# Late eigenvalue powers four to seven on GpSimd in the half-block loop of an S5 layer

## The chip, the cores and the metric

The kernel runs on one core of a Trainium2 chip. The core has a TensorE (PE, with its weight loads shown as PEld), a VectorE (DVE), a ScalarE (ACT) and a GpSimd (POOL); transfers are issued from the queues of SyncE (SP), ACT and GpSimd. Each engine runs its own instructions in order, and the engines wait for one another by semaphores. The metric is the device time of one launch in microseconds; with several runs, the median counts.

## The reference

One layer over 1024 latent tokens and 256 context tokens with 1024 channels: an S5 mixer (64 groups of 16 channels, 64 complex states each, two directions, the latent scan starting from the context's final state), GELU and a gated linear unit, then a SwiGLU feed-forward, with RMS norms and modulation by a condition. Cut to what matters here:

```python
def s5_direction(u_ctx, u_lat, lam_re, lam_im, log_step, b_re, b_im, c_re, c_im):
    lam = lax.complex(lam_re, lam_im)
    lam_bar = jnp.exp(lam * jnp.exp(log_step)[:, None])
    b_bar = ((lam_bar - 1.0) / lam)[..., None] * lax.complex(b_re, b_im)
    c_mat = lax.complex(c_re, c_im)

    def run(u, h0):
        bu = jnp.einsum('lgh,gnh->lgn', u, b_bar)
        bu = bu.at[0].add(lam_bar * h0)
        a = jnp.broadcast_to(lam_bar, bu.shape)
        _, h = lax.associative_scan(_linear_combine, (a, bu), axis=0)
        return jnp.einsum('lgn,ghn->lgh', h, c_mat).real, h[-1]

    y_c, h_c = run(u_ctx, zeros)
    y_l, _ = run(u_lat, h_c)
    return y_c, y_l
```

## The kernel before

Time is cut into chunks of T = 8 tokens (32 context chunks, 128 latent ones). Inside a chunk everything is matrix products with powers of the eigenvalues, `lam_bar` to the 1st up to the 8th, kept in `PW` (eight complex rows of 64 groups on 128 partitions: both directions times 64 states). From chunk to chunk runs a scan over the chunk states.

**The half-block loop** (`for hb in range(16)`, from line 698) makes these chunk states. The 64 groups are eight blocks of eight; a half block is one block in one direction. For each half block there is

- `bl_make`: two products of the input matrix with the powers, two 128x1024 instructions, on GpSimd for the half blocks in `PMUL` (1, 3, 5, 6, 8, 10, 13) and on the VectorE for the others; made six half blocks ahead;
- `bl_sum` (L433): the two products added, by an accumulating DMA that GpSimd's queue issues; five half blocks ahead. Since the queue is in order, this issue waits there until both products exist;
- `bl_tr` (L443): eight transposes on PE, copied to SBUF by ACT (L446), with `bb_copy` (L451); two half blocks ahead;
- `sums` (L584): 32 products on PE, in two halves of 16, copied by ACT (L590, L592, L593) into the states `STQ`, four buffers of 20 KB per partition in the region `RA`;
- `pair`: the states combined two by two, in four 128x256 instructions, on GpSimd (temporaries `ptmp`, KB 2 and 3 of the region `RXc`) for the half blocks in `PPAIR`, else on the VectorE; one half block later;
- `u_ctx`, `rs_lat`, `u_act`: the input's norm and modulation, on GpSimd (the context of a block, two 128x256 instructions), VectorE and ACT. `UCTX` says in which half block which block's context comes; `sums(8)` is the first to use block 4;
- `ctx_tree` on the VectorE: the scan over the 32 context chunks.

`sums`, `bl_tr` and `pw_full` take their PSUM banks from one ring of two (`pv2`). The order of all this is written out by hand: the order of the source is the order in each engine's queue.

**The powers.** Before the loop the VectorE makes the rows 0, 1, 3 and 7 of `PW` (powers 1, 2, 4, 8). Row 2 (power 3) is `pw_mul(PW[:, 2:3], ...)` in half block 3, rows 4, 5 and 6 (powers 5, 6 and 7) come from two calls in half block 4. A call is four GpSimd instructions: two products into two temporaries, a subtraction and an addition. `pw_full(0)` and `pw_full(1)` turn rows 0 to 3 and 4 to 7 on PE (eight products, L386), and ACT copies the result to `PWF` (L388), which is first read by the output matrices `cl_ops` on GpSimd from half block 12 on. `PW` shares its place with the end of the last state buffer, which `sums(12)` is the first to write, and the temporaries of `pw_mul` lie in the third state buffer, which `sums(8)` is the first to write.

**Behind the loop** come the last `pair` on GpSimd, the rest of the output matrices, `ctx_last`, and the scan over the latent chunks (`scan`, on the VectorE, one step after another), beside which GpSimd and PE make output matrices and Toeplitz kernels (`k_mats`, turned by a DMA through DRAM into `KQ`). Then follow the mixer's output, the gated unit and the feed-forward.

Of the kernel before, what the change touches and what calls it, by code (L numbers as in the profile page):

```python
# [24 lines left out]
G = 64  # L25
# [17 lines left out]
def s5_ffn_kernel(tc, a, out):  # L43
# [3 lines left out]
    with ctx:  # L47
        ctx.enter_context(tc.manual_schedule())
        sb = ctx.enter_context(tc.tile_pool(name="sb", bufs=1))
        def region(tag, kb, dt=F32):  # L50
            return sb.tile([P, int(kb * 256)], dt, tag=tag, name=tag)

        def view(reg, kb, shape, parts=P):
            off = int(round(kb * 256))
            n = int(np.prod(shape))
            v = reg[:parts, off:off + n]
            if len(shape) > 1:
                names = "abcdef"[:len(shape)]
                v = v.rearrange(f"p ({' '.join(names)}) -> p {' '.join(names)}",
                                **{k: d for k, d in zip(names, shape)})  # L60
            return v
# [3 lines left out]
        RA = region("ra", 80.5)  # L65
        RU = region("ru", 40)
        RC = [region(f"c{i}", 16) for i in range(4)]
        RXa, RXc = region("rxa", 8), region("rxc", 8)
        RW = region("rw", 6)

        def bc(ap, axis, n):
            sh = list(ap.shape)
            sh.insert(axis, n)
            return ap.unsqueeze(axis).to_broadcast(sh)

        def tt(o, x, y, op, eng=V):
            eng.tensor_tensor(out=o, in0=x, in1=y, op=op)  # L77
# [69 lines left out]
        def pv2():  # L147
            return pW.tile([P, 2, 512], F32, tag="v", name="pv", bufs=2)
# [46 lines left out]
        def ada1(h, *ks):  # L195
            for k in ks:
                for b in range(2):
                    i = 2 * b + h
                    PE.matmul(prow[32 * i:32 * i + 2], scs[:, k], stage[h][k][:, b], start=k == 0, stop=k == 7, tile_position=(0, 32 * i))
# [141 lines left out]
        def pw_mul(o, x, y):  # L341

            m = x.shape[1]
            a_, b_ = (view(RA, kb, [m, 2, G]) for kb in (42, 43))
            yr, yi = (bc(bc(y[:, i], 1, 2), 1, m) for i in range(2))
            tt(a_, x, yr, MUL, E)
            tt(b_, x[:, :, ::-1], yi, MUL, E)
            tt(o[:, :, 0], a_[:, :, 0], b_[:, :, 0], SUB, E)
            tt(o[:, :, 1], a_[:, :, 1], b_[:, :, 1], ADD, E)
# [4 lines left out]
        def power8():  # L354

            pt = pv2()[:, 0, 0:128].rearrange("p (r q d e) -> p r q d e", r=2, q=8, d=2)
            for gp in range(2):
                for d in range(2):
                    sl = slice(64 * d, 64 * d + 64)
                    PE.matmul(pt[64 * gp:64 * gp + 64, :, :, d], ident[:, sl],  # L360
                              PW[:, 7].rearrange("p r (q e t) -> p r q e t", q=8, t=2)[:, :, :, :, gp], start=True, stop=True)
            pt = pt.rearrange("p r q d e -> p r (q d e)")
            S.copy(SQ[0][:, 0::2], pt)
            S.activation(SQ[0][:, 1], pt[:, 1], AF.Copy, scale=-1.0)
            S.copy(LQ[0], SQ[0])
# [16 lines left out]
        def pw_full(n):  # L382
            pt = pv2()[:, 0].rearrange("p (t i d a) -> p t i d a", t=4, i=2, d=2)
            for gp in range(2):
                for d in range(2):
                    PE.matmul(pt[64 * gp:64 * gp + 64, :, :, d], ident[:, 64 * d:64 * d + 64], PW[:, 4 * n:4 * n + 4, :, gp::2],  # L386
                              start=True, stop=True)
            S.copy(PWF[:, 4 * n:4 * n + 4], pt)  # L388
# [48 lines left out]
        def bl_tr(hb, copy=True):  # L437
            b, d = bd(hb)
            t1 = bls(hb)[0]
            pt, w_ = pv2(), Win[hb % 3]  # L440
            for j in range(2):
                for i in range(4):
                    PE.transpose(pt[:, j, P * i:P * i + P], t1[:, 4 * j + i].rearrange("p s h -> p (s h)"), ident)  # L443
            if not copy:
                return pt, w_
            S.copy(w_.rearrange("p j i n -> p (j i n)"), pt.rearrange("p j n -> p (j n)"))  # L446
            bb_copy(hb)
# [7 lines left out]
        def mix_rows():  # L455
            S.copy(r4, prow.rearrange("p (m n) -> p m n", m=4))

        def mix_turn():
            for m in range(4):
                PE.transpose(prow[:, P * m:P * m + P], r4[:, m], ident)  # L460

        def mix_scale(h):

            hs, pt = slice(4 * h, 4 * h + 4), prow.rearrange("p (m n) -> p m n", m=4)
            for r in range(2):
                tt(cb[:, r, :, hs], pt.rearrange("p m (b j q) -> p b j m q", b=2, j=2)[:, :, h, :, r], modb[:, 0:2, hs], ADD)
            stt(cb[:, :, 1, hs], cb[:, :, 1, hs], 1.0, bc(nrm[:, 0, hs], 1, 2), ADD, MUL)
            for r in range(2):
                tt(mx[:, r].rearrange("p b (j g) -> p b j g", g=T), bc(cb[:, r, :, hs], 3, T), bc(bc(msk, 1, 4), 1, 2), MUL)
# [107 lines left out]
        def sums(hb):  # L577
            b, d = bd(hb)
            for j in range(2):
                w, pv = Win[hb % 3][:, j], pv2()  # L580
                for ri in range(2):
                    for i in range(4):
                        c0 = 160 * (i // 2)
                        PE.matmul(pv[64 * (i % 2):64 * (i % 2) + 64, ri, c0:c0 + 160], w[:, i, 64 * ri:64 * ri + 64],  # L584
                                  U[:, 8 * b + 4 * j + i], start=True, stop=True)
                pv = pv[:, :, 0:320].rearrange("p r (e c) -> p c r e", e=2)
                e = 8 * (b % 2) + 4 * d + 2 * j
                st = STQ[b // 2][:, :, :, e:e + 2]
                if d == 0:
                    S.copy(st, pv)  # L590
                else:
                    S.copy(st[:, 159:31:-1], pv[:, 32:160])  # L592
                    S.copy(st[:, 31::-1], pv[:, 0:32])  # L593
# [88 lines left out]
        PPAIR = (3, 5, 7, 8, 9, 11, 12, 13, 15)  # L682
        UACT = {1: (2, 0, 4), 2: (2, 4, 8), 3: (3, 0, 4), 4: (3, 4, 8)}
        UACT.update({6 + i: (4 + i // 2, 4 * (i % 2), 4 * (i % 2) + 4) for i in range(8)})
        UCTX = {1: 2, 3: 3, 6: 4, 7: 5, 9: 6, 11: 7}
        RSL = {0: 2, 1: 3, 3: 4, 5: 5, 6: 6, 8: 7}
        ADA1 = {0: (0, 1), 1: (2, 3, 4), 2: (5, 6, 7)}
        ADA2 = {10: 12, 11: 14, 12: 16, 13: 18, 15: 22}
# [9 lines left out]
        for hb in range(16):  # L698
            sums(hb)
            ada1(1, *ADA1.get(hb, ()))  # L700
            if hb == 0:
                power8()
            if hb == 3:
                mix_rows()
            for n in BLTR.get(hb, (hb + 2,)):
                if n < 16:
                    bl_tr(n)
            if hb == 3:
                mix_turn()
            if hb == 4:  # L710
                mix_scale(1)
                mix_sel(1)
            if hb in RSL:
                rs_lat(RSL[hb])
            if hb == 4:
                mix_cols(1)
                tq = pA.tile([P, 512], F32, tag="r3", name="tq")
                LQ += [t[:, o_:o_ + 192].rearrange("p (r e) -> p r e", e=G) for t, o_ in ((tq, 0), (tq, 192), (LTb, 256))]
            if hb == 0:
                tt(Xc[:, 16:], ctxT[:, 16:], bc(rcp, 1, G - 16), MUL)  # L720
            if hb == 1:
                powers(0)
            if hb == 2:
                powers(1)
                SY.dma_start(BXY[:, 1], a["bxy"][:, 3])
            if hb in UACT:
                u_act(*UACT[hb])
            if hb in UCTX:
                u_ctx(UCTX[hb])
            if hb >= 1:  # L730
                pair(hb - 1, E if hb - 1 in PPAIR else V)
            if hb == 5:
                powers(2, 3)
            for a_ in CTREE.get(hb, ()):
                ctx_tree(*a_)
            if hb + 6 in (7, 9, 11, 12, 14, 15):
                lb_psum(hb + 6)
            bl_sum(hb + 5)
            bl_make(hb + 6)
            if hb == 3:  # L740
                pw_mul(PW[:, 2:3], PW[:, 0:1], PW[:, 1])
                tt(KD.rearrange("p q g h -> p (q g) h"), bc(pat, 1, 8), bc(dcol, 2, HC), MUL, E)
            if hb == 4:
                pw_mul(PW[:, 4:6], PW[:, 0:2], PW[:, 3])
                pw_mul(PW[:, 6:7], PW[:, 2:3], PW[:, 3])
            if hb in (6, 8):
                pw_full(hb // 2 - 3)
            if hb == 9:
                cs_load(0)
            if hb == 11:  # L750
                V.tensor_copy(LQ[4], SQ[4])
                cs_sign(0)
            for _ in range(CLAT.get(hb, 0)):
                CL0.pop(0)()
            ada_load(ADA2.get(hb, 0))
# [1004 lines left out]
```

## Time and profile before

| | us |
|---|---|
| median of 3 runs | 1024.42 (1023.78 to 1026.05) |
| the profiled execution | 1022.42 |
| its span, first to last instruction | 1020.6 |
| busy: PE, DVE, ACT, POOL | 961.9, 785.5, 436.5, 766.5 |
| loop, first sums to the last state copy | 40.0 to 122.4 |
| scan on the VectorE | 127.65 to 227.5 |

How to read it: a profile is one execution. A row of a timeline has the start, the duration, the engine, the line, the operation, the tile written and those read, the shape, the number of instructions merged into the row, and in brackets the idle time before it with what released it. Most helpers record their instructions at line 77 (`tt`), so the tiles tell them apart: `ru` is the input, `ra` holds states and powers, `rxc` the temporaries, `c` the four 16 KB regions, `pv` the PSUM ring. A row of waits has the waiting engine and line, what it waited for, the total, the number of times and the longest.

### The profile page before, as it was taken

The page shows a single profiled execution, that of the slowest core. Times are in us where ns is not written, and L with a number is a line of the kernel's source. Part 1 is how long each engine was busy: PE and PEld are TensorE (multiplying, and loading weights), DVE is VectorE, ACT ScalarE, POOL GpSimd, SP SyncE. Part 2 cuts the span into 40 slices and gives each one's busy share as a digit, 9 for nine tenths or more (in the row PEclk, how much of TensorE's full clock was granted, in tenths as well). Part 3 has the DMA queues.
Part 4 walks back from the last instruction along what each step waited for, and adds up shares of the span by engine and source line. Part 5 has one row for each costly group of instructions (what it writes and reads, how often), then busy time and mean ns, then how long its engine had stood idle before and what let it go on. Part 6 is the DMA issues. An engine that isn't in the chain of part 4 may idle for free. (4 is left out here: it accounts for less than half of the span.)

```text
span 1020.6 us, 18545 instructions
## 1 busy us (share of the span) xinstructions
PE 961.9 (94%) x6988; PEld 771.8 (76%) x6988; DVE 785.5 (77%) x1642; ACT 436.5 (43%) x854; POOL 766.5 (75%) x590
## 2 busy tenths in 40 slices
PE   5987798779999999999999999999999999999996
PEld 1466423668999987878888888888888888888885
DVE  7979799994365777997958768585958778686987
ACT  5477622234454663523334343424343343324337
POOL 5799899991682548979786877778686877777674
PEclk9999999989999999999999999999999999999999
DMA  9764997323612021011212112121212111121205
GB/s 335 276 139 91 298 341 231 91 74 89 227 61 83 2 104 62 22 42 42 83 41 74 39 45 62 42 73 52 73 42 82 39 40 58 42 73 52 73 22 165
DMA packets 48546, 98.95 MB, mean 97 GB/s; under 512 B 4285, under 2 KB 18877, under 8 KB 47177
## 3 DMA queue, kind: packets, MB, share of 16 engines
q1 hardware_dynamic: 43272, 86.64, 25.9%
q0 software_dynamic: 2016, 7.34, 3.8%
q10 hardware_dynamic: 3168, 3.79, 1.1%
q8 instruction: 55, 0.90, 0.4%
q14 instruction: 35, 0.28, 0.1%
HBM read 84.25 MB, written 6.17 MB: 89 GB/s over the span
## 5 line engine op out<-in xcount | busy, mean ns | idle before, releaser
L77 POOL TENSOR_TENSOR c<-rxc,c 128x512 fp32r<-128x512 f32 x128 | 170.0, 1342 | 55.6 <-ACT c L1227 53.7
L1286 PE MATMUL ut<-ra,c 128*128 128x512 f32 x400 | 155.8, 390 | 0.5 <-ACT ra L1227 0.3
L1287 PE MATMUL ut<-ra,c 128*128 128x512 f32 x400 | 155.7, 389 | 0.3 <-DVE ra L77 0.3
L1288 PE MATMUL ut<-ra,c 128*128 128x512 f32 x400 | 155.7, 389 | 0.0
L1227 ACT CAST c<-rxc 128x512 fp32r<-128x512 f32 x128 | 79.0, 622 | 146.4 <-PE xt L1568 51.8
L1568 PE MATMUL xt<-c,c 128*128 128x512 f32 x540 | 129.7, 389 | 0.0
L77 DVE TENSOR_TENSOR ru<-ru,xt 128x1024 f32<-128x1024 f32 x90 | 107.8, 1216 | 12.9 <-PE xt L1568 9.1
L1568 PEld LDWEIGHTS xt<-c,c 128*128 128x128 f32 x540 | 101.4, 188 | 21.0
L77 DVE TENSOR_TENSOR ru<-ut,ru 128x512 f32<-128x512 f32 x98 | 67.2, 686 | 42.4 <-PE ut L1288 36.9
L1286 PEld LDWEIGHTS ut<-ra,c 128*128 128x128 f32 x400 | 75.1, 188 | 16.7 <-ACT ra L1227 0.8
L1287 PEld LDWEIGHTS ut<-ra,c 128*128 128x128 f32 x400 | 75.1, 188 | 16.2 <-issue 0.6
L1288 PEld LDWEIGHTS ut<-ra,c 128*128 128x128 f32 x400 | 75.1, 188 | 15.9 <-POOL c L77 0.3
L77 POOL TENSOR_TENSOR c<-rw,c 128x512 fp32r<-128x512 f32 (+1 forms) x29 | 39.8, 1372 | 37.3 <-ACT c L1227 36.6
L77 POOL TENSOR_TENSOR c<-ru,c 128x512 fp32r<-128x512 f32 (+1 forms) x39 | 58.0, 1487 | 9.3 <-ACT c L1227 4.9
L1288 PE MATMUL ut<-c,c 128*128 128x512 f32 x160 | 62.4, 390 | 1.3 <-POOL c L77 1.3
L1287 PE MATMUL ut<-c,c 128*128 128x512 f32 x160 | 62.3, 389 | 0.0
L1286 PE MATMUL ut<-c,c 128*128 128x512 f32 x160 | 62.2, 389 | 0.0
L77 POOL TENSOR_TENSOR rxc<-rxc 128x512 f32<-128x512 f32 x40 | 60.9, 1523 | 1.6
L1568 PE MATMUL ut<-c,c 128*128 128x512 f32 x216 | 51.9, 389 | 0.0
L584 PE MATMUL pv<-ru,c 128*64 128x160 f32 x512 | 43.7, 312 | 7.3 <-POOL ru L77 2.6
L77 DVE TENSOR_TENSOR pe<-pe,ru 128x256 f32<-128x256 f32 x64 | 27.4, 429 | 29.5 <-ACT pe L1127 17.4
L77 DVE TENSOR_TENSOR ru<-ru,ut 128x512 f32<-128x512 f32 x76 | 47.3, 680 | 0.3
(427 smaller groups left out, 2568.2 us busy)
## 6 DMA issues: line engine op xcount, KB each, us to landing
c<-in_ada_w SPq DMA_DIRECT2D x46, 256.0 KB
rxc<-in_w SPq DMA_DIRECT2D x38, 256.0 KB
rxc<-in_w SPq DMA_DIRECT2D x19, 512.0 KB
ru<-in_w SPq DMA_DIRECT2D x11, 512.0 KB
rw<-in_w SPq DMA_DIRECT2D x11, 512.0 KB
ra<-in_ada_w SPq DMA_DIRECT2D x10, 512.0 KB
ra<-in_ada_w SPq DMA_DIRECT2D x18, 256.0 KB
ru<-in_xT SPq DMA_DIRECT2D x4, 1024.0 KB
```

Of the source, the lines that this page charges most:

```text
L77: eng.tensor_tensor(out=o, in0=x, in1=y, op=op)
L584: PE.matmul(pv[64 * (i % 2):64 * (i % 2) + 64, ri, c0:c0 + 160], w[:, i, 64 * ri:64 * ri + 64], U[:, 8 * b + 4 * j + i], start=True, stop= ...
L1227: S.copy(o[0], x)
L1286: PE.matmul(pu, wh, bh, start=start, stop=False)
L1287: PE.matmul(pu, wh, bl, start=False, stop=False)
L1288: PE.matmul(pu, wl, bh, start=False, stop=stop)
L1568: PE.matmul(pd, w[:, cs_], b, start=j in (1, 2, 4) and n == 0, stop=n == 2, skip_group_check=j not in (1, 2, 4))
```

## The change

`pw_mul` takes its temporaries from KB 2 and 3 of `RXc` instead of `RA`. Row 2 of the powers, and with it the instruction for the skip term `KD`, moves from half block 3 to 7; rows 4 to 6 move from 4 to 9; `pw_full(0)` and `pw_full(1)` move from the ends of half blocks 6 and 8 to those of 10 and 11. `u_ctx(4)` moves from half block 6 to 5. No instruction is added or taken away.

```diff
         def pw_mul(o, x, y):
 
             m = x.shape[1]
-            a_, b_ = (view(RA, kb, [m, 2, G]) for kb in (42, 43))
+            a_, b_ = (view(RXc, kb, [m, 2, G]) for kb in (2, 3))
...
-        UCTX = {1: 2, 3: 3, 6: 4, 7: 5, 9: 6, 11: 7}
+        UCTX = {1: 2, 3: 3, 5: 4, 7: 5, 9: 6, 11: 7}
...
             bl_sum(hb + 5)
             bl_make(hb + 6)
-            if hb == 3:
+            if hb == 7:
                 pw_mul(PW[:, 2:3], PW[:, 0:1], PW[:, 1])
                 tt(KD.rearrange("p q g h -> p (q g) h"), bc(pat, 1, 8), bc(dcol, 2, HC), MUL, E)
-            if hb == 4:
+            if hb == 9:
                 pw_mul(PW[:, 4:6], PW[:, 0:2], PW[:, 3])
                 pw_mul(PW[:, 6:7], PW[:, 2:3], PW[:, 3])
-            if hb in (6, 8):
-                pw_full(hb // 2 - 3)
+            if hb in (10, 11):
+                pw_full((10, 11).index(hb))
             if hb == 9:
                 cs_load(0)
```

## The prediction

> **What bounds the kernel now.** I began with the page, then the windows that follow the stages, then the waits of each engine in the half-block loop, and last the timeline of that loop engine by engine. The profiled execution took 1022.42 us, 1.8 us more than its span.
>
> ```profile
> span 1020.6 us, 18545 instructions
> ...
> 59.50:125.40 65.90, 51.63 (x529) 38.81 (x529) 52.44 (x145) 50.08 (x110) 64.41 (x82) 0.97 0.71 177
> 69.50:110.40 40.90, 33.00 (x334) 25.52 (x334) 38.90 (x101) 31.49 (x68) 39.80 (x56) 0.96 0.58 124
> 110.40:122.40 12.00, 9.62 (x109) 7.60 (x107) 5.28 (x20) 9.63 (x23) 11.84 (x14) 1.00 1.03 345
> 127.65:227.50 99.85, 83.63 (x1512) 48.12 (x1504) 97.75 (x508) 26.46 (x55) 96.80 (x66) 0.96 0.59 188
> 262.00:1020.60 758.60, 747.03 (x3736) 633.40 (x3730) 563.02 (x790) 314.74 (x617) 554.36 (x402) 1.00 0.19 61
> ```
>
> Columns after the length: busy PE, PEld, DVE, ACT, POOL, then granted clock, DMA share, GB/s. From 262 us the TensorE is full (747 of 759), so a delay at its start comes out at the end. From 127.65 to 227.5 the VectorE runs the serial scan without a pause, so a later start of the scan is a later end. The question is thus one number: how far does the start of the scan move? In the loop before it, GpSimd is full (64.4 of 65.9) and the VectorE nearly so until 110.4 (38.9 of 40.9); then the VectorE idles (5.3 of 12) and waits for states that PE and ACT make.
>
> ```profile
> DVE r L483 <- PE prow L476: 0.8, 1, 0.8
> ...
> PE pv L584 <- POOL ru L77: 2.6, 1, 2.6
> PE pv L584 <- ACT rxa L388: 1.8, 2, 0.9
> ...
> POOL rw L77 <- DMA c<-rw: 2.4, 1, 2.4
> ```
>
> The first row is the only wait of weight that the VectorE has between 69 and 111: nothing the change moves releases it. The second is PE waiting for the context of block 4 (two GpSimd instructions), the third PE waiting for the two copies of the eigenvalue powers. The last is GpSimd's only wait for anybody from 59 to 128, and it comes behind the loop.
>
> **GpSimd's queue, step by step.** Here are the rows of GpSimd that carry the change (start, duration):
>
> ```profile
> 68.61 1.84 POOL L77 TENSOR_TENSOR ra<-ra 128x128 f32<-128x128 f32 x4
> 70.41 0.40 POOL L77 TENSOR_TENSOR r<-r 128x128 f32<-128x128 f32 x1
> 70.77 1.29 POOL L77 TENSOR_TENSOR rxc<-ra,r 128x256 f32<-128x256 f32 x2
> ...
> 78.08 4.27 POOL L77 TENSOR_TENSOR ra<-ra 128x256 f32<-128x256 f32 x8
> 82.30 0.87 POOL L433 DMA_DIRECT2D c<-rxc  x1
> 82.91 1.60 POOL L77 TENSOR_TENSOR ru<-ru,r 128x256 f32<-128x256 f32 x2
> ...
> 89.37 0.88 POOL L433 DMA_DIRECT2D c<-c  x1
> ...
> 96.93 0.87 POOL L433 DMA_DIRECT2D c<-rxc  x1
> ...
> 101.84 0.88 POOL L433 DMA_DIRECT2D c<-c  x1
> 102.45 1.59 POOL L77 TENSOR_TENSOR rxc<-ra,r 128x256 f32<-128x256 f32 x2
> ...
> 105.46 0.88 POOL L433 DMA_DIRECT2D c<-c  x1
> ...
> 123.63 1.81 POOL L77 TENSOR_TENSOR ra<-ra,rxc 128x256 f32<-128x256 f32 x2
> ```
>
> From start to start, the four products of half block 3 take 1.80 us (68.61 to 70.41), the skip-term product behind them 0.36, the eight of half block 4 4.22 (78.08 to 82.30). All three, 6.38 us, leave their places. GpSimd would then reach the accumulating transfer of half block 12 (issued at 89.37) at 82.99; that block 4's context (82.91, 1.60) goes one half block ahead changes the order there, not this sum. But the transfer adds two operands that the VectorE makes:
>
> ```profile
> 85.23 2.35 DVE L77 TENSOR_TENSOR c<-c,tq 128x1024 f32<-128x1024 f32 x2 [0.19 <-issue]
> ```
>
> They are done at 85.23 + 2.35 = 87.58, and by the waits above nothing lets the VectorE be sooner. The issue sits in GpSimd's queue in order, so GpSimd now stands idle for some 4.6 us, until 87.6, and behind the waiting issue stand all its further products, pairs and transfers. Of 6.38 us taken out it keeps 1.77 as a lead. In half block 7 come back 1.80 + 0.36 (0.4 us late from there), in half block 9, behind the transfer of 14, the 4.22: from half block 10 on GpSimd is **4.6 us late**. It had no idle time left to make this good. Three things follow.
>
> First, the pairs. The last pair of the loop ended at 123.63 + 1.81 = 125.44; now 130.05. The scan's first addition reads what it wrote:
>
> ```profile
> 128.05 0.29 DVE L77 TENSOR_TENSOR ra<-ltb,ra 128x128 f32<-128x128 f32 x1
> ```
>
> So the scan starts at least 130.05 - 128.05 = 2.0 us later, whatever PE does.
>
> Second, the powers. Their second turn on PE with its copy moves from half block 8 to 11, between the transposes of 13 and the sums of 12, and it needs the eight products, which end where the pair of 102.45 begins: 102.45 + 4.6 = 107.05.
>
> ```profile
> 76.20 1.13 PE L386 MATMUL pv<-ra,r 128*64 128x256 f32 x8
> ...
> L388 ACT COPY rxa<-pv x2: 560/566/571, 79.0 to 92.1; 128x512 f32<-128x512 f32 x2
> ...
> 103.58 1.09 PE L443 MATMUL pv<-r,c 128*128 128x128 f32 x8 [1.07 <-ACT ra L593]
> 104.60 1.31 PE L584 MATMUL pv<-ru,c 128*64 128x160 f32 x16
> 109.81 1.06 PE L443 MATMUL pv<-r,c 128*128 128x128 f32 x8 [1.20 <-DMA c<-c]
> 114.40 1.09 PE L443 MATMUL pv<-r,c 128*128 128x128 f32 x8 [1.07 <-ACT ra L593]
> ...
> 108.16 1.27 ACT L590 COPY ra<-pv 128x640 f32<-128x640 f32 x2
> ```
>
> PE issues in order: with the transposes of 13 done near 103.7 it stands until 107.2, then 1.13 for the powers (108.3), then the sums of 12 in two halves of 1.31 (109.6 and 110.9; the second needs the bank that the copy of 0.57 frees, in time). The state copies of 12 end near 111.6 instead of 108.16 + 1.27 = 109.4, and the transposes of 14 start at 110.9 instead of 109.81: **+1.1** at full clock. From there PE and ACT hand each other two banks and the delay stays.
>
> But PE has stood still for 3.5 us. The one like gap in this loop (PE idle from 82 to 84) was followed by this:
>
> ```profile
> 82.00:84.00 2.00, 0.00 (x0) 0.00 (x0) 1.90 (x7) 1.94 (x5) 1.92 (x5) 1.00 0.17 33
> 84.00:86.00 2.00, 1.43 (x12) 1.28 (x14) 1.74 (x7) 0.82 (x3) 2.00 (x4) 0.52 1.03 197
> 86.00:88.00 2.00, 2.00 (x22) 1.85 (x20) 2.00 (x4) 0.72 (x1) 1.92 (x4) 0.63 0.22 41
> ...
> 84.57 3.80 PE L584 MATMUL pv<-ru,c 128*64 128x160 f32 x32 [2.60 <-POOL ru L77]
> ...
> 62.93 2.39 PE L584 MATMUL pv<-ru,c 128*64 128x160 f32 x32
> ```
>
> The granted clock fell to 0.52 and 0.63, and the same 32 products took 3.80 instead of 2.39: 1.4 us. With that the second path gives 1.1 + 1.4 = **+2.5**; I take it, since the new gap is longer than the one measured. The Trainium skill's page "TensorE: Matmul & The Clock Gate" (Part 1, the HAM clock gate) has the clock halved after about one free-running window of 3.4 us without work. By it a gap of 2.6 us need not have been enough, and the trace shows that it was. If by that rule the clock stays whole after the new gap, this path is +1.1, the pairs' +2.0 decides, and the time is 1026.4.
>
> Third, the accumulating transfers. That of 13 moves from 96.93 to 97.3, that of 15 from 105.46 to 110.05.
>
> ```profile
> DMA to landing us min/median/max: 4.5/5.3/8.8
> ...
> SPq L520 <- DMA c<-c: 4.5, 1, 4.5
> ```
>
> With the median of 5.3 the one of 15 lands at 115.4, before the transposes of 15 are due (114.40 + 1.1 to 2.5), so it costs nothing; with 8.8 it lands at 118.85, 4.45 after 114.40. The longest landings were under the modulation weights that SP loads from 102.6 on; but SP's queue then stands 4.5 us for this very landing, so a later transfer should find the DMA engines emptier, and I take the median. The Trainium skill's page "DMA: Bandwidth & Descriptors" (Anatomy of one DMA, SWDGE path) fits 2.0 us plus bytes over 436e3, an estimate of 3.2 us for these 512 KB. No landing here is under 4.5, so the measurement decides; by the page the larger rival below would vanish.
>
> **What I cost at nothing.** The context of block 4 now runs before PE needs it: this takes away the 2.6 us wait and 1.4 us of slow clock, and the powers' turns at 76 and 89 us free PE of 1.8 us of waits. PE runs ahead from half block 8, but the lead ends in half block 11, where the transposes of 13 need the transfer that lands at 97.3 + 5.3 = 102.6 (they began at 103.58), and then the powers; meanwhile the VectorE, full until 110.4, could not use it. The new temporaries are the two KB that GpSimd's own pairs use, in order on one engine: no wait. The same region is loaded again behind the loop by ACT's queue, which now waits for the last pair until 130.05; behind it on ACT stands a clearing copy that waited for the VectorE anyway. GpSimd's lateness also goes on into the output matrices; its wait of 2.4 for a transfer takes some of it.
>
> ```profile
> 214.39 3.92 PE L945 MATMUL pw<-ra,ru 128*128 128x128 f32 x16 [2.98 <-DMA ra<-kd]
> ...
> 227.66 0.49 PE L922 MATMUL pe<-c,ra 64*64 64x128 f32 x4 [1.55 <-DVE ra L77]
> ```
>
> There PE waits for kernels made from these matrices, and later 1.55 us for the scan: if all 4.6 us arrive, this path gives 4.6 - 1.55 = +3.05.
>
> **The sum.** Scan start +2.5 us, between +2.0 and +3.05: the profiled execution of the changed kernel 1022.42 + 2.5 = 1024.9. This profile lies 2.0 below the median of the runs, so the median goes from 1024.42 to **1026.9**, with 1026.4 to 1027.5 as this case's own range.
>
> **Rivals.**
> A larger loss: the transfer of 15 lands late (8.8 us), +4.45, and with a second slow clock of 1.4 after the wait +5.85: 1028.9 to 1030.3. For it: two loaded landings near 8 us. Against it: SP stands still then.
> No change: GpSimd's lag comes out smaller. The last pair may be 128.05 - 125.44 = 2.6 us late before the scan feels it; if the VectorE were done with its operands for half block 12 some 2 us sooner, or GpSimd's instructions ran quicker after its idle stretch, the time would be 1024.4. Against it: the VectorE has no wait there that could vanish.
> Faster: the early context is what decides. PE's 2.6 and 1.4 us at half block 8 are carried to the end of the loop: 1024.42 - 4.0 = 1020.4, or 1022.4 if half is. It decides if GpSimd issues the transfer of 15 before 105.46. For it: this is the longest wait of PE in the loop. Against it: GpSimd's queue, above, has 4.22 us of products ahead of that issue.
>
> **Numbers.** A difference under 0.2% (2.05 us) can't be told from none here. Forecast 0.60; its range lies at or above 1026.47, and I put 0.50 there and 0.10 below for the scatter of a median; larger loss 0.15; no change 0.12; faster 0.13. So slower 0.65, same 0.10 + 0.12 = 0.22, faster 0.13. The range runs from 1024.0 (no change) to 1030.0 (most of the larger loss) and leaves out the gain and a little of the loss.
>
> **What would show it.** In the changed profile: GpSimd idle for 4 to 5 us before its transfer near 87.6, released by a VectorE product; eight products near 103 to 107; PE waiting for them about 3.5 us ahead of the second turn of the powers, with a granted clock near half behind it; the last pair ending near 130; the scan starting near 130.2. I am wrong if GpSimd does not idle before 88, or if the scan starts before 128.5.

## The result, and the profile after

| | before | after |
|---|---|---|
| median of 19 runs each, us | 1024.17 (1022.87 to 1026.05) | 1026.3 (1025.34 to 1028.3) |
| profiled execution, us | 1022.42 | 1027.71 |
| its span, us | 1020.6 | 1025.9 |

The ratio is 1.0022, with a 95% interval of 1.0016 to 1.0029: 2.2 us more, between 1.6 and 3.0. The forecast was 2.5 us more, 1026.9 within 1026.4 to 1027.5. The growth holds (1024.42 and 2.2 are 1026.6), though the median of 1026.3 lies 0.1 below that range, and whether the growth passes the 0.2% that the prediction takes as the least difference, the interval doesn't settle. Two steps of the reasoning were wrong, the landing of one transfer and the reason for PE's slow clock, and it takes the experiments to see that.

First the timeline of GpSimd in the changed kernel (start, duration, operation, tiles, in brackets the idle time before it and what ended it):

```profile
82.80 1.61 POOL L77 TENSOR_TENSOR ru<-ru,r 128x256 f32<-128x256 f32 x2
88.98 0.88 POOL L433 DMA_DIRECT2D c<-c  x1 [4.58 <-DVE ltb L77]
...
103.94 1.70 POOL L77 TENSOR_TENSOR rxc<-ra 128x256 f32<-128x256 f32 x2
...
108.28 1.29 POOL L77 TENSOR_TENSOR rxc<-ra,r 128x256 f32<-128x256 f32 x2
...
111.00 0.87 POOL L433 DMA_DIRECT2D c<-c  x1
...
129.17 1.80 POOL L77 TENSOR_TENSOR ra<-ra,rxc 128x256 f32<-128x256 f32 x2
```

Idle time that GpSimd didn't have here before stands in the second row: 4.58 us ahead of the transfer of half block 12. What it waited for are the VectorE's products for that transfer:

```profile
86.00 2.35 DVE L77 TENSOR_TENSOR c<-c,tq 128x1024 f32<-128x1024 f32 x2 [0.19 <-issue]
...
132.00 0.29 DVE L77 TENSOR_TENSOR ltb<-ra,lta 128x128 f32<-128x128 f32 x1
...
132.40 0.29 DVE L77 TENSOR_TENSOR ra<-ltb,ra 128x128 f32<-128x128 f32 x1
```

They end at 88.35, and the issue comes 0.63 us later. The scan begins at 132.00 (second row; 127.65 before). Now PE:

```profile
69.50 0.43 PE L475 MATMUL ltb<-ra,r 128*128 128x64 f32 x2 [1.06 <-DVE ra L77]
...
103.62 1.08 PE L443 MATMUL pv<-r,c 128*128 128x128 f32 x8 [2.73 <-DMA c<-rxc]
108.26 1.98 PE L386 MATMUL pv<-ra,r 128*64 128x256 f32 x8 [3.55 <-POOL ra L77]
110.02 3.00 PE L584 MATMUL pv<-ru,c 128*64 128x160 f32 x32
112.96 1.09 PE L443 MATMUL pv<-r,c 128*128 128x128 f32 x8
...
118.78 1.07 PE L443 MATMUL pv<-r,c 128*128 128x128 f32 x8 [2.26 <-DMA c<-c]
```

PE waits 3.55 us for the eight products ahead of the second turn of the powers, and the turn and the sums of 12 behind it take 1.98 + 3.00. The three rows of L443 are the transposes of half blocks 13, 14 and 15. The last of them waits 2.26 us for the transfer of 15, a wait that this place didn't have in the profile of before. The windows of that stretch (columns as in the prediction; the first is 1 us long):

```profile
104.00:105.00 1.00, 0.70 (x7) 0.45 (x5) 1.00 (x4) 0.20 (x1) 1.00 (x3) 0.77 0.19 20
...
106.00:108.00 2.00, 0.00 (x0) 0.00 (x0) 1.83 (x6) 1.55 (x5) 1.84 (x6) 0.50 0.99 273
108.00:110.00 2.00, 1.74 (x8) 1.01 (x10) 1.93 (x7) 0.00 (x0) 1.92 (x4) 0.50 1.02 228
...
112.00:114.00 2.00, 2.00 (x26) 1.61 (x22) 0.00 (x0) 1.42 (x2) 1.92 (x4) 1.00 1.05 405
```

The granted clock falls between 104 and 105, while the transposes of 13 run, and is at 0.50 from before the turn until 110. The DMA engines are full from 106 on, and the transfer of 15, issued at 111.00, falls into that. Its landing, from the answer for that issue alone, in the changed kernel and then in the kernel before:

```profile
DMA to landing us min/median/max: 7.6/7.6/7.6
```

```profile
DMA to landing us min/median/max: 8.8/8.8/8.8
```

So the longest landing of the view in the prediction, 8.8, was that of this very transfer: issued at 105.46, landed at 114.26, and its transposes began at 114.40. It had 0.14 us to spare.

**Three stretches that hold the loop's difference.** The profiles of these two kernels also differ by up to 1.5 us in where the loop stands in the span. I therefore measure from the row of L475 above (68.72 in the profile of before):

```profile
68.72 0.43 PE L475 MATMUL ltb<-ra,r 128*128 128x64 f32 x2 [1.06 <-DVE ra L77]
```

From there run three stretches: to the start of the transposes of 14, from there to those of 15, and from there to the first instruction of the scan. Each is a difference of starts in one trace. The table has all profiles, the experiments told below among them:

| kernel | to transposes of 14 | to those of 15 | to the scan | sum | ratio of times |
|---|---|---|---|---|---|
| before | 41.09 | 4.59 | 13.25 | 58.93 | |
| before, second | 41.24 | 4.59 | 13.25 | 59.08 | |
| before, third | 41.26 | 4.94 | 13.22 | 59.42 | |
| after | 43.46 | 5.82 | 13.22 | 62.50 | 1.0022 |
| after, second | 43.86 | 5.73 | 14.10 | 63.69 | 1.0022 |
| after, third | 44.05 | 4.63 | 13.25 | 61.93 | 1.0019 |
| all products ahead of the transfer | 40.95 | 4.81 | 13.22 | 58.98 | 0.9999 |
| four products ahead of it | 42.25 | 5.64 | 14.10 | 61.99 | 1.002 |
| transfer of 15 sooner | 44.45 | 4.64 | 13.26 | 62.35 | 1.0031 |
| PE kept busy, 22 | 43.82 | 6.18 | 13.39 | 63.39 | 1.0025 |
| PE kept busy, 12 | 43.12 | 6.82 | 13.68 | 63.62 | 1.0018 |
| both | 43.37 | 4.63 | 13.25 | 61.25 | 1.0005 |
| before, transfers sooner | 40.17 | 4.62 | 13.25 | 58.04 | 0.9981 |

The first stretch is PE's wait for the powers and the slow clock: 41.2 on average before, 43.8 after (43.46, 43.86 and 44.05), **+2.6**. The second is 4.6 when PE is released by ACT's copies, and more when the transfer of 15 is late: +1.2, +1.1 and 0 in the three profiles of after. The third is 13.25 unless the clock falls again behind that wait (up to 14.10). In the runs with four products and with PE kept busy the clock was slow at L475 already (its row takes 0.69 us in place of 0.43 in the run with four, the next one 0.74 in place of 0.44), which puts 0.3 to 0.5 us into their first stretch (their transfer of 12 is issued 19.8 to 20.0 us after L475, against 19.5 in the three profiles of after). Each line is one execution.

### The profile page after: what moved, and what is told of

It is laid out like the page before. It is cut to its first block, busy times and chain, and to the rows that moved or that the text cites. A ratio compares the mean times of both kernels' runs of the same rounds, so it can differ in the third digit from the quotient of the medians.

```text
span 1025.9 us, 18545 instructions
## 1 busy us (share of the span) xinstructions
PE 963.5 (94%) x6988; PEld 773.3 (75%) x6988; DVE 786.4 (77%) x1642; ACT 436.8 (43%) x854; POOL 766.3 (75%) x590
## 5 line engine op out<-in xcount | busy, mean ns | idle before, releaser
L77 POOL TENSOR_TENSOR c<-rxc,rxa 128x1024 f32<-128x1024 f32 x23 | 46.9, 2119 | 0.1
```

## The experiments

The theory: GpSimd's idle time ahead of the transfer of 12 makes all behind it late, and this reaches the scan through PE's wait for the powers, through the transfer of 15, or both. The rivals: the context of block 4 one half block sooner does something by itself; the new places of the products cost by themselves; only one of the two ways matters.

**The early context alone.** On the kernel before:

```diff
-        UCTX = {1: 2, 3: 3, 6: 4, 7: 5, 9: 6, 11: 7}
+        UCTX = {1: 2, 3: 3, 5: 4, 7: 5, 9: 6, 11: 7}
```

> Only the context of block 4 one half block sooner; the powers stay where they were. My theory (the VectorE and the accumulating transfers set the loop's end, so PE's wait of 2.6 us before the sums of 8 is covered): the wait of PE and the slow clock behind it vanish in the profile, the scan starts where it started, time 1024.2 within 0.8. Rival (PE's wait is carried to the end): 1020.2 to 1022.2.

Measured: 1024.66, ratio 1.0004 (0.9995 to 1.0013). Its one profiled execution took 1497.59 us at a mean clock of 0.593 and isn't read, so this run doesn't show that the wait is gone; in the profile of the changed kernel, which has the same line, the sums of 8 start without a wait. By the times, taking away PE's longest wait of the loop is worth nothing that can be measured: the rival that it decides is out.

**The products where GpSimd would idle.** The changed kernel, with all twelve products and the skip term in half block 7, ahead of its transfer:

```diff
-            bl_sum(hb + 5)
-            bl_make(hb + 6)
             if hb == 7:
                 pw_mul(PW[:, 2:3], PW[:, 0:1], PW[:, 1])
                 tt(KD...)
-            if hb == 9:
+            if hb == 7:
                 pw_mul(PW[:, 4:6], PW[:, 0:2], PW[:, 3])
                 pw_mul(PW[:, 6:7], PW[:, 2:3], PW[:, 3])
+            bl_sum(hb + 5)
+            bl_make(hb + 6)
```

> The changed kernel, but all twelve products and the skip term stand in half block 7 ahead of the accumulating transfer of 12, where GpSimd had its new idle time of 4.6 us. My theory (GpSimd's idle time, 4.6 us of queue lost, is the cause): GpSimd does not idle before 90, issues the transfer of 15 near 105.5 after the loop's start as before, and the loss is gone: 1024.2 within 1.0. Rival (the late turns of the powers on PE, or the earlier context, cost by themselves): 1025.5 to 1026.5.

Measured: 1024.44, ratio 0.9999 (0.999 to 1.0008). GpSimd's one wait from 59 to 131 us, then rows of its timeline, the last product and the transfer of 12, then PE's:

```profile
POOL rw L77 <- DMA c<-rw: 3.0, 1, 3.0
```

```profile
89.57 0.60 POOL L77 TENSOR_TENSOR ra<-rxc 128x64 f32<-128x64 f32 x2
90.13 0.88 POOL L433 DMA_DIRECT2D c<-c  x1
```

```profile
103.04 1.94 PE L443 MATMUL pv<-r,c 128*128 128x128 f32 x8 [2.06 <-DMA c<-rxc]
104.91 1.98 PE L386 MATMUL pv<-ra,r 128*64 128x256 f32 x8
106.67 3.42 PE L584 MATMUL pv<-ru,c 128*64 128x160 f32 x32
110.54 1.07 PE L443 MATMUL pv<-r,c 128*128 128x128 f32 x8 [0.45 <-DMA c<-c]
```

The products are still three to four half blocks later than before, with the new temporaries and the late turns on PE, and the loss is gone. They now fill the time in which GpSimd stood, and the transfer needs no wait (90.13). So it is not their lateness that costs, but the empty queue ahead of a blocked issue: shown. One more thing is to be seen: the clock was slow here as well (1.98 and 3.42, as in the changed kernel), after the wait of 2.06 for the transfer of 13, and it cost nothing: the powers started at 104.91 and not at 108.26, and behind the sums the transposes of 14 still waited 0.45 us for their transfer. Here the slow clock had room; in the changed kernel it comes on top of the wait and has none.

**The transfer of 15 ahead of the eight products.** The changed kernel, with that issue moved from half block 10 to 9:

```diff
-            bl_sum(hb + 5)
+            if hb != 10:
+                bl_sum(hb + 5)
...
             if hb == 9:
+                bl_sum(15)
                 pw_mul(PW[:, 4:6], PW[:, 0:2], PW[:, 3])
```

> The changed kernel, but the accumulating transfer of 15 is issued in half block 9 ahead of the eight products instead of behind them; the products end 0.6 us later. Theory A (the late landing of 15 set the end in the changed profile, where the transposes of 15 waited 2.3 us for it): that wait goes, 1025.0 to 1025.6. Theory B (PE's wait for the products and the slow clock behind it set the end, as predicted): 1026.3 to 1026.9, by the 0.6.

Measured: 1027.94, ratio 1.0031 (1.002 to 1.0042). PE:

```profile
108.22 1.98 PE L386 MATMUL pv<-ra,r 128*64 128x256 f32 x8 [3.04 <-POOL ra L77]
...
113.00 1.09 PE L443 MATMUL pv<-r,c 128*128 128x128 f32 x8
...
117.64 1.09 PE L443 MATMUL pv<-r,c 128*128 128x128 f32 x8 [1.08 <-ACT ra L593]
```

This misses both expectations, which ended at 1026.9. The wait for the transfer is gone (second stretch 4.64), but the products stand behind one more issue, and the first stretch is 44.45. The loop, 62.35, is no shorter than the changed kernel's on average (62.7). That the transfer of 15 alone makes the loss is out. The profiled execution, 1025.4 us, is the shortest of the seven, so what made the others longer than the changed kernel isn't shown.

**PE kept busy ahead of the powers.** The changed kernel, with 22 products of the identity with itself ahead of the second turn; their result is overwritten:

```diff
-            pt = pv2()[:, 0].rearrange("p (t i d a) -> p t i d a", t=4, i=2, d=2)
+            pt = pv2()[:, 0]
+            for _ in range(22 * n):
+                PE.matmul(pt[:, 0:128], ident, ident, start=True, stop=True)
+            pt = pt.rearrange("p (t i d a) -> p t i d a", t=4, i=2, d=2)
```

> The changed kernel, with 22 extra products of the identity ahead of the second turn of the powers, into the bank that the turn then overwrites, so that PE works through its wait of 3.6 us for GpSimd. The granted clock stays at 1.00 and the turn and the sums of 12 take 1.1 and 2.4 to 2.6 us instead of 2.0 and 3.0. Theory B (the slow clock is on the path): 1.3 us faster than the changed kernel, 1025.0. Theory A (the landing of 15 sets the end): PE waits longer at the transposes of 15 instead, time 1026.3 within 0.4.

Measured: 1026.74, ratio 1.0025 (1.0014 to 1.0036). PE (lines behind the edit are 3 higher in this kernel):

```profile
106.65 5.08 PE L385 MATMUL pv<-r 128*128 128x128 f32 x44
111.66 1.13 PE L389 MATMUL pv<-ra,r 128*64 128x256 f32 x8
...
121.07 1.18 PE L446 MATMUL pv<-r,c 128*128 128x128 f32 x8 [2.62 <-DMA c<-c]
```

Each of the 22 shows as two records, and together they took 5.08 us and held the turn up until 1.3 us behind the end of GpSimd's products (110.34). The clock is whole (1.13 for the turn, against 1.98), but what it gave went into the overrun, and the profiled execution is the longest of the twelve (1029.92 us): this run can't tell the theories apart.

**The changed kernel, second profile.**

> The changed kernel again, unaltered, for a second execution under the profiler and more times. In the first profile the stretch from the modulation's product on PE (start of the L475 row, 69.50) to the scan's first instruction (132.00) took 62.5 us against 58.9 before, 3.6 more, while the median grew by 2.1. If the loop's end varies from execution to execution with the landing of the transfer of 15 (7.6 us in the first profile), the second shows another landing and a stretch of 61 to 62; if not, 62.5 again and the rest is given back behind the scan.

Measured: 1027.25, ratio 1.0022 (1.0012 to 1.0032): the same loss again. Its loop takes 63.69 us, which is neither of the two expected. The first two stretches agree with the first profile; in the third, transposes in a slow clock add 0.85.

**Four products ahead of the transfer, eight behind.** The changed kernel, where only row 2 of the powers and the skip term stand ahead of the transfer of 12:

```diff
-            bl_sum(hb + 5)
-            bl_make(hb + 6)
             if hb == 7:
                 pw_mul(PW[:, 2:3], PW[:, 0:1], PW[:, 1])
                 tt(KD...)
+            bl_sum(hb + 5)
+            bl_make(hb + 6)
             if hb == 9:
```

> The changed kernel, but the four products and the skip term (2.2 us) stand in half block 7 ahead of the transfer of 12, in GpSimd's idle time; the eight products stay in half block 9. GpSimd's lag from half block 10 on falls from 4.6 to 2.4 us: the eight products end near 105.7 instead of 108.2, PE waits about 1.2 us for them and its clock stays full. Theory B (PE's wait and slow clock): sums of 12 end as before the change, 1024.2 within 0.7. Theory A (the landing of 15, issued 2.4 us later than before the change): plus 1.1, 1025.3.

Measured: 1026.23, ratio 1.002 (1.001 to 1.003), which misses both expectations. GpSimd, then PE:

```profile
89.40 0.88 POOL L433 DMA_DIRECT2D c<-c  x1 [3.25 <-PE pv L584]
```

```profile
102.30 1.09 PE L443 MATMUL pv<-r,c 128*128 128x128 f32 x8
106.78 1.91 PE L386 MATMUL pv<-ra,r 128*64 128x256 f32 x8 [3.39 <-POOL ra L77]
...
111.65 1.09 PE L443 MATMUL pv<-r,c 128*128 128x128 f32 x8
...
117.29 1.94 PE L443 MATMUL pv<-r,c 128*128 128x128 f32 x8 [2.08 <-DMA c<-c]
```

```profile
105.00:106.00 1.00, 0.00 (x0) 0.00 (x0) 0.97 (x4) 1.00 (x4) 0.92 (x3) 1.00 1.02 250
106.00:108.00 2.00, 1.23 (x6) 0.74 (x8) 1.86 (x6) 0.23 (x1) 1.84 (x5) 0.72 1.08 228
```

GpSimd still stood for 3.25 us. The row names PE's sums, but as in the changed kernel it was the VectorE's products that came last, at 88.76, 0.64 us ahead of the issue; from L475 they are 0.5 us later than there, by the slow clock at L475. The 2.16 us that GpSimd got done ahead of its wait come back as 1.5 us in the first stretch (43.8 to 42.25), and those 0.5 us are most of the rest. But PE was at the powers sooner too and waited as long as ever, 3.39; the clock, whole until then, fell at the end of this wait (the windows); and the transfer of 15 was late all the same (second stretch 5.64, third 14.10). I had expected the gain to come through whole.

**PE kept busy, with 12 products in place of 22.** The edit is as above with `12 * n`.

> As e_warm, but with 12 extra products: in e_warm the 22 took 5.1 us in the profile (106.65 to 111.7) and ran past the end of GpSimd's products (110.3) by 1.3 us, so they cost what they gained. Twelve should end 0.7 us before GpSimd does. Theory B (slow clock on the path): 1.3 us under the changed kernel, 1025.0. Theory A (landing of 15): 1026.3, with a longer wait at the transposes of 15.

Measured: 1026.66, ratio 1.0018 (1.0008 to 1.0027). PE, then GpSimd's last product:

```profile
105.00 3.50 PE L385 MATMUL pv<-r 128*128 128x128 f32 x24
108.43 1.13 PE L389 MATMUL pv<-ra,r 128*64 128x256 f32 x8
...
111.66 1.09 PE L446 MATMUL pv<-r,c 128*128 128x128 f32 x8
...
118.48 1.07 PE L446 MATMUL pv<-r,c 128*128 128x128 f32 x8 [3.27 <-DMA c<-c]
```

```profile
106.97 0.59 POOL L77 TENSOR_TENSOR ra<-rxc 128x64 f32<-128x64 f32 x2
```

The clock is whole at the turn, and the turn with the sums takes 3.2 us, down from the 4.7 of the changed kernel (108.43 to 111.66 against 108.26 to 112.96). But twelve overran too: they ended at 108.50, GpSimd at 107.56, so 0.9 us of the 1.5 are spent again, where the expectation had them end 0.7 us early. The first stretch is 0.3 shorter than in the first profile (43.12 against 43.46). That gain doesn't reach the scan: the transfer of 15 took 8.0 us, and the wait for it is 3.27, up from 2.26. This looks like two paths of about one length: whoever cures one sees nothing.

**The kernel before, with two transfers sooner.** On the kernel before:

```diff
-            bl_sum(hb + 5)
+            if hb < 9:
+                bl_sum(hb + 5)
             bl_make(hb + 6)
+            if hb in (8, 9):
+                bl_sum(hb + 6)
```

> The kernel before, with only the two last accumulating transfers issued sooner: that of 14 at the end of half block 8, that of 15 at the end of half block 9 (each behind the making of its operands), ahead of the context and the pairs instead of behind them. The transposes of 14 then no longer wait 1.2 us. My theory (the loop's end hangs on these landings and on PE and ACT, so they are worth something by themselves): 0.5 to 1.0 us faster than before, 1023.2 to 1023.7. Rival (PE and ACT alone set it): 1024.2.

Measured: 1023.14, ratio 0.9981 (0.9969 to 0.9993): faster than both, 1.9 us under the kernel before as it ran beside it. PE:

```profile
108.89 1.09 PE L443 MATMUL pv<-r,c 128*128 128x128 f32 x8 [1.07 <-ACT ra L590]
...
113.51 1.09 PE L443 MATMUL pv<-r,c 128*128 128x128 f32 x8 [1.07 <-ACT ra L593]
```

Both waits are for ACT alone, and the first stretch is 40.17: the kernel before had lost a microsecond to the transfer of 14. Where the rest of the 1.9 comes from isn't shown.

**The kernel before, second and third profile.**

> The kernel before again, unaltered, for another execution under the profiler. From the L475 row of PE (68.72) to the scan's first instruction (127.65) its first profile has 58.9 us; behind the scan's start come 893.0 us. The changed kernel has 62.5 and 63.7 us in two profiles, 3.6 and 4.8 more, while medians differ by 2.2. If the first profile of before was a quick execution of the loop, this one shows 59.5 to 60.5; if not, 58.9 again, and the difference lies ahead of the loop or behind it.

> The kernel before once more, for a third execution under the profiler: the stretch from the L475 row to the scan's first instruction 59.5 to 60.5 if the first profile was a quick execution, 58.9 if it was not.

Measured: one execution each, 1022.96 and 1023.53. The loops take 59.08 and 59.42: the first agrees with 58.9, the second lies between the two expectations. In the third profile the transposes of 15 waited 1.38 us for their transfer, which took 9.5 us and came 0.35 us late (4.94); and the clock was slow behind a wait of 1.96 us for the transfer of 13 (the sums of 12 took 4.00 us), with a first stretch no longer for it (41.26).

**Both cures.** The changed kernel with the transfer of 15 issued ahead of the products and with the 12 products on PE.

> The changed kernel with both cures at once: the transfer of 15 ahead of the eight products, and 12 extra products of the identity that keep PE's clock up. Alone neither helped (e_sum15 1.0031, e_warm12 1.0018, the changed kernel 1.0022). If two paths of nearly one length end the loop (PE's wait for the products with the slow clock, and the late transfer of 15), each hides the other's cure and both together gain 0.9 to 1.4 us: stretch from L475 to the scan 61.0 to 61.6, time some 1025.2. If something else ends it (GpSimd's last pair), the stretch stays at 62.3 or more.

Measured: 1025.55, ratio 1.0005 (0.9994 to 1.0017). PE, GpSimd and the VectorE:

```profile
112.13 1.09 PE L446 MATMUL pv<-r,c 128*128 128x128 f32 x8
...
116.76 1.09 PE L446 MATMUL pv<-r,c 128*128 128x128 f32 x8 [1.07 <-ACT ra L596]
```

```profile
128.50 1.81 POOL L77 TENSOR_TENSOR ra<-ra,rxc 128x256 f32<-128x256 f32 x2
```

```profile
130.41 0.29 DVE L77 TENSOR_TENSOR ra<-ltb,ra 128x128 f32<-128x128 f32 x1
```

Each cure alone left the loop at 62.35 and 63.62 us; the two together take 1.5 us off that of the changed kernel (62.7 on average, 61.25 here), though the 12 products overran here too (they took 4.81 us and ended at 108.97, GpSimd at 108.36). That is how two parallel paths behave, and the times go the same way. It is one profile for each run, though: the shortest of the three of the changed kernel, 61.93, is only 0.7 longer, and the interval of the ratio overlaps with that of the 12 products alone. The last pair ends at 130.31, 0.10 before the addition that reads it. So the third path, the pairs, is now the next to bind.

**The changed kernel, third profile.**

> The changed kernel a third time. The stretch from L475 to the scan's first instruction was 62.5 and 63.7 us in two profiles, against 58.9, 59.1 and 59.4 in three of the kernel before: 3.1 to 4.8 more, where the medians of the times differ by 2.2 (1.6 to 2.9). If the two profiles of the changed kernel were slow executions, this one shows 61 to 62 and a time near 1026.3; if the loop really loses 3 to 5 us in every execution, it shows 62.5 to 63.7 again, and something gives a part back in runs without a profile.

Measured: 1026.59, ratio 1.0019 (1.001 to 1.0028). PE, and the granted clock (the column ahead of the last two) in windows of 1 us:

```profile
102.19 1.94 PE L443 MATMUL pv<-r,c 128*128 128x128 f32 x8 [2.29 <-DMA c<-rxc]
107.32 1.98 PE L386 MATMUL pv<-ra,r 128*64 128x256 f32 x8 [3.19 <-POOL ra L77]
...
112.57 1.09 PE L443 MATMUL pv<-r,c 128*128 128x128 f32 x8
...
117.20 1.09 PE L443 MATMUL pv<-r,c 128*128 128x128 f32 x8 [1.07 <-ACT ra L593]
```

```profile
99.00:100.00 1.00, 0.90 (x14) 0.61 (x10) 0.76 (x3) 0.24 (x3) 0.92 (x3) 1.00 1.10 213
100.00:101.00 1.00, 0.00 (x0) 0.00 (x0) 1.00 (x2) 0.71 (x2) 1.00 (x3) 1.00 1.07 201
101.00:102.00 1.00, 0.00 (x0) 0.00 (x0) 1.00 (x2) 0.00 (x0) 0.92 (x2) 0.65 0.45 82
```

Here the slow clock came early and the transfer landed sooner (6.9 us), so the wait for it vanished, and the loop, 61.93 as the expectation had it, is still 2.8 us longer than the 59.1 of before: that is PE's path by itself.

## Why the prediction was right, and where it was wrong

**GpSimd's queue: right.** Forecast: idle some 4.6 us ahead of the transfer of 12, and 4.6 us late from half block 10 on. Measured: idle 4.58, and the transfer of 15 comes 111.00 - 69.50 = 41.50 us after L475 against 105.46 - 68.72 = 36.74, so 4.76 us late. The run with all products ahead of the transfer shows that this idle time is the cause. Two terms of 0.6 us were missing and left the idle time as it was: GpSimd came to the issue 84.41 - 69.50 = 14.91 us after L475, not 82.99 - 68.72 = 14.27, and the issue came 0.63 us after its operands and not at once.

**Second consequence, the powers: right in its sum, and it carries the result; wrong in why the clock falls.** Forecast: PE waits 3.5 us, a clock near half behind it, +2.5 to the transposes of 14. Measured: 3.55 (2.56 and 3.19 in the second and third profile), clock 0.50, +2.6. I had put the clock down to this wait alone ("but PE has stood still for 3.5 us"). In none of the three profiles is that so. In the first the clock falls between 104 and 105, while the transposes of 13 run, and the wait begins only at 104.71. In the second and third, and with all products ahead, it falls in the wait for the transfer of 13, to which PE now comes sooner (waits of 2.86, 2.29 and 2.06 us; 0.69, 0.65 and 0.51 in the windows of 1 us in which it falls). The run with four products shows that the wait for the powers can do it too: there the transposes of 13 didn't wait, and the clock fell at the end of 3.39 us. So the term of 1.4 us for a slow clock came out partly by luck: another wait had made it slow before. By the rule of the Trainium skill (the page "TensorE: Matmul & The Clock Gate", Part 1) the halving needs about one window of 3.4 us without work, and the window runs free. The traces agree that the place shifts from run to run, but in the third profile the clock fell less than 2 us after PE went idle near 100, in a gap of 2.29 us; a whole window of 3.4 us without work was not needed there.

**Third consequence, the transfers: wrong.** The step "with the median of 5.3 the one of 15 lands at 115.4, ... so it costs nothing" failed. The landing took 7.6, 7.9 and 6.9 in the three profiles of after and, in the runs with four products ahead and with 12 on PE, 7.6 and 8.0, never near the median. By the prediction's own terms, 110.05 + 7.6 = 117.65 is 0.75 later than the 116.9 at which its transposes were due, which makes +3.25 out of +2.5. The row was there to be asked: the 8.8 of the quoted view was this transfer. I had argued that SP's queue stands still then; the windows show the DMA engines full from 106 to 114. The larger loss thus came true in part: the wait exists in two of three profiles, at 1.1 to 1.2 us and not 4.45, because the landing took 7.6 and 7.9 in place of 8.8 and PE's path had used up most of the same time. The Trainium skill's fit (the page "DMA: Bandwidth & Descriptors", Anatomy of one DMA, SWDGE path) would give an estimate of 3.2 us for these 512 KB; every landing here is above that, so the measurement decides.

**First consequence, the pairs: right, and not what decided.** The floor of +2.0 was there (the last pair ends at 130.97, 1.43 before the addition at 132.40), but PE's paths were longer. It comes next: with both cures the loop is +2.1 over the 59.1 of before.

**What was costed at nothing: right.** The early context gave nothing (1.0004), and no row shows GpSimd waiting for the new temporaries. The lateness that goes on into the output matrices did not decide: from the scan's start to the end it is 892.95, 893.65 and 893.69 us in the profiles of before and 893.9, 892.77 and 893.45 in those of after.

**What stays open.** The loop is 2.8 to 4.6 us longer in the three profiles of after, while the medians differ by 2.2. The prediction named 1024.9 us for the profiled execution and a scan starting near 130.2; it was 1027.71 and 132.00, and from L475 the scan comes 3.0 to 4.8 us later than in the profile that the prediction worked from, where +2.5 was forecast. That the median comes out so near is therefore in part luck. The three profiled executions of before were short ones (1022.42 to 1023.53, with medians from 1024.02 to 1024.63), two of the three of after were long ones (1027.71 and 1028.26), and single executions of one kernel spread over some 3 us. So the profiles may bring the ends of both spreads together, and how often the wait for the transfer of 15 comes in an ordinary execution wasn't measured. By the times, +2.5 was right within the interval; whether it is PE's path alone in most executions isn't settled.

## What to carry to other kernels

Work that sits ahead of a transfer in an engine's in-order queue may be what fills the wait for that transfer's operands; taken out, it leaves a hole, and the same work put in later makes all behind it late. Before a transfer's landing is costed by a median, ask for the landing of that very transfer and for its slack (here 8.8 us and 0.14 us). When a cure of a visible wait gives nothing, cure the next wait along with it before giving the theory up: two paths of one length hide each other's cures.

## What the hardware showed that was not expected

- The granted clock of PE fell to 0.65 between 1 and 2 us after the last product before 100 us (third profile of after), and in the run with all products ahead of the transfer it was down after a wait of 2.06 us; in the first profile of after the transposes behind a wait of 2.73 us still took 1.08, at full speed. The length of a gap alone doesn't tell.
- The accumulating transfer of 512 KB for half block 12, issued ahead of SP's modulation weights, landed in 4.5 to 5.2 us in every profile. That of 15, issued beside these weights, took 6.9 to 9.5 us, and up to 10.8 us where 14 and 15 were issued together (the run with both cures).
- A transfer that had waited for the VectorE was issued 0.63 us after its operands' last instruction ended.
- A product of the 128x128 float32 identity with itself shows as two records. At a whole clock 22 of them took 5.08 us; at a clock of 0.50 for most of the time 12 took 4.81 (the run with both cures).
